# Nine products of lead for the two adding-DMA blocks of a Strassen group, and one more tile in the weight ring

## The chip, the cores and the metric

One NeuronCore of a Trainium2 chip runs the whole program in one launch. The metric is the device time of one execution in microseconds, lower is better; the median of three timed executions of the kernel before is 2247.82 us.

## The reference, cut to what matters

Two residual blocks over 512 tokens of width 1024, in fp32. The first holds an HGRN2 mixer and a dilated attention, each followed by a feed-forward network (FFN); the second a mixer of sparse attention and gated linear attention, and a third FFN. All three FFNs have this form, with `d_ff` 2816:

```python
def swiglu_ffn(u, w_in, w_down):
    gate, up = jnp.split(u @ w_in, 2, axis=-1)
    return (jax.nn.silu(gate) * up) @ w_down
```

`u` is the normalised state (512 x 1024), `w_in` is 1024 x 5632. So the up-projection gives 22 pairs of a gate tile and an up tile, each tile 128 columns wide.

## The kernel before, in words

**Arithmetic.** fp32 products are made of three fp32r matmuls. Each operand is split into a *head* (the value rounded to fp32r by ScalarE's CAST) and a *rest* (value minus head), and `mm3` sums rest times head, head times head and head times rest in PSUM. A weight block that is used must therefore stand in SBUF as a head and a rest.

**The three up-projections** (`ffn`). The first five pairs of a FFN (`FC`) are made by plain products through `gemm`. The other 17 (6 in the first half of the FFN, 11 in the second) are made by Strassen's method in groups, one pair each (`strassen`). A group has seven products, a1, b1, a2, b2, c, a3, a4, each with its own 128 x 512 weight block (a linear combination of the four quarters) and 12 matmuls of 128 x 256. The order is written out as slots in `S_AT`: a1 0, b1 1, a2 3, b2 4, c 5, a3 6, a4 9, so that a4 of a group stands at slot 2 of the next; the last group of a half goes by `S_LAST`: a1 0, b1 1, a2 3, b2 4, a3 5, c 6, a4 7. There are 51 groups, 357 products, 4284 matmuls. The products a1 to a4 of a group accumulate in one PSUM bank; behind each, ScalarE copies the bank out (behind a1 and a2, `COPY G`), or VectorE reads it. `b2` and `c` are added into `G` by VectorE and put through silu by ScalarE.

**The weights** (`Weights`). A group's blocks come from three loads on SP's queue: r4 (512 KB, two quarters), r1 and r3 (256 KB each). VectorE makes the sums from them with five adds (`sums_1`, `sums_2`: adds 1 and 2 into the second halves of r1 and r3, adds 3 and 4 into r2). `heads(i)` is one 128 x 1024 CAST for two products, `rests(i)` their subtract on VectorE. For two products the rest is made in another way (`rest_dma`): ScalarE writes the negated head, and a DMA issued by GpSimd adds the raw block from HBM to it (line 339; 256 KB, 102 of them). These two are c and a4. So heads(3) casts c and a3 together, and rests(3) issues c's DMA and subtracts for a3; `last` makes a4's block.

**The order of the preparation.** Each step stands in a list with a due time: the slot of the product that uses it, less a lead, in steps of `SLOT` (1.44 us). Before a product is issued, `advance` issues all that is due; a step issues first the loads of its group that are not yet issued. The leads before: sums 7 and 6 ahead of a1, heads(1) 5, rests(1) 4, heads(2) and rests(2) 6 and 5 ahead of a2, heads(3) and rests(3) 6 and 5.9 ahead of c, `last` at a1 itself. All tiles (128 x 1024 fp32) come from one ring of `ROOM` = 12; a load that takes a used tile waits until the last use of that tile is over. Instructions of an engine run in the order in which they were issued, so a load that waits holds up the loads behind it on SP's queue.

Most element-wise instructions are recorded at one line (L249, a helper), so the rows are told apart by engine and by the program's tile names: `w_raw` is a raw block, `w` a head or a rest, `G` and `h` the gate and up results, `ps` a PSUM bank, `E` the activations' operands.

Of the kernel before, what the change touches and what calls it, by code (L numbers as in the profile page):

```python
# [78 lines left out]
def strassen_order(n):  # L79

    at = [(7 * g + t, g, p) for g in range(n) for p, t in (S_AT if g < n - 1 else S_LAST).items()]
    return [(g, p) for _, g, p in sorted(at)]
# [101 lines left out]
class Clock:  # L184
# [3 lines left out]
    def __init__(self, hop):  # L188
        self.hop = hop
        self.free = {"pe": 0.0, "v": 0.0, "a": 0.0, "g": 0.0}  # L190
        self.written, self.read = {}, {}
        self.held = []
# [68 lines left out]
class Weights:  # L261
# [1 line left out]

    ROOM, HELD = 12, 3
    TILE, SLOT = 0.68, 1.44

    def __init__(self, prog, ctx, aps):
# [71 lines left out]
    def group(self, grp):  # L341
        n, aps, t, split, at, v = grp["n"], grp["aps"], grp["tiles"], grp["split"], grp["at"], self.v
        first, second = slice(0, n), slice(n, 2 * n)

        def load(name, sl, ap):
            def go():
                t[name] = self.tile(F32)
                self.nc.sync.dma_start(t[name][:, sl], ap)
            return go

        def add(o, osl, x, xsl, y, ysl):
            v.tensor_add(t[o][:, osl], t[x][:, xsl], t[y][:, ysl])

        def sums_1():
            add("r1", second, "r4", second, "r4", first)
            add("r3", second, "r1", first, "r4", second)

        def sums_2():
            t["r2"] = self.tile(F32)
            add("r2", first, "r1", first, "r1", second)  # L360
            add("r2", second, "r3", first, "r2", first)

        def heads(i):
            def go():
                t["h%d" % i] = self.tile()
                self.a.copy(t["h%d" % i][:, :2 * n], t["r%d" % i][:, :2 * n])
            return go

        def rests(i):
            def go():  # L370
                h, l = t["h%d" % i], self.tile()
                t["l%d" % i] = l
                if i == 3:
                    self.rest_dma(l[:, first], h[:, first], aps[2])
                    self.sub(v, l[:, second], t["r3"][:, second], h[:, second])
                else:
                    self.sub(v, l[:, :2 * n], t["r%d" % i][:, :2 * n], h[:, :2 * n])
                self.free(t, "r%d" % i)
                for p, sl in zip(((), ("a1", "b1"), ("a2", "b2"), ("c", "a3"))[i], (first, second)):
                    split[p] = h[:, sl], l[:, sl]  # L380
            return go

        def last():
            t["l4"] = self.tile()
            hi, lo = t["l4"][:, second], t["l4"][:, first]
            self.a.copy(hi, t["r4"][:, first])
            self.rest_dma(lo, hi, aps[0][:, first])
            split["a4"] = hi, lo
            self.free(t, "r4")

        u = len(self.units)
        self.loads += [[load("r4", slice(0, 2 * n), aps[0]), u], [load("r1", first, aps[1]), u], [load("r3", first, aps[2]), u]]
        s = self.SLOT
        for use, lead, what in (
            ("a1", 7, sums_1), ("a1", 6, sums_2), ("a1", 5, heads(1)), ("a1", 4, rests(1)), ("a2", 6, heads(2)), ("a2", 5, rests(2)),
            ("c", 6, heads(3)), ("c", 5.9, rests(3)), ("a1", 0, last),
        ):
            self.todo.append((at[use] - lead * s + 0.01, u, what, len(self.loads)))

# [43 lines left out]

    def product(self, p):

        _, grp, name = self.units[self.at]
        assert p == name, (self.at, p, name)
        self.now = grp["at"][p]
        self.advance()
        r = grp["split"].pop(p)  # L450
        self.at += 1
        if p in ("b1", "b2", "a3", "a4"):
            self.free(grp["tiles"], *{"b1": ("l1", "h1"), "b2": ("l2", "h2"), "a3": ("l3", "h3"), "a4": ("l4",)}[p])
        return r


class Program:
    def __init__(self, tc, ctx, I, O):
        self.tc, self.nc, self.I, self.O = tc, tc.nc, I, O
        nc = self.nc  # L460
        self.clock = Clock(0.5)
        self.v, self.a = Timed(nc.vector, "v", self.clock), Timed(nc.scalar, "a", self.clock)
        self.g, self.t = Timed(nc.gpsimd, "g", self.clock), Timed(nc.tensor, "pe", self.clock)
        PS = bass.MemoryType.PSUM
        self.const = ctx.enter_context(tc.tile_pool(name="const", bufs=1))
        self.p2 = ctx.enter_context(tc.tile_pool(name="p2", bufs=28))
        self.p4 = ctx.enter_context(tc.tile_pool(name="p4", bufs=26))
        self.small = ctx.enter_context(tc.tile_pool(name="small", bufs=24))
        self.ps_p = ctx.enter_context(tc.tile_pool(name="ps", bufs=8, space=PS))
        self.bg, self.hooks, self.evq = [], deque(), []  # L470
        self.after_norm = None
# [60 lines left out]
    def mm3(self, out, a, b, first, last):  # L532

        self.t.matmul(out, a[1], b[0], start=first, stop=False, skip_group_check=True)
        self.t.matmul(out, a[0], b[0], start=False, stop=False, skip_group_check=True)
        self.t.matmul(out, a[0], b[1], start=False, stop=last, skip_group_check=True)

    def mm(self, out, a, b, first=True, last=True):
        self.t.matmul(out, a, b, start=first, stop=last, skip_group_check=True)
# [1048 lines left out]
    def strassen(self, X, afters):  # L1588


        banks = {}
        for g, p in strassen_order(len(afters)):
            key = g, p[0]
            first = key not in banks
            if first:
                banks[key] = self.ps((128, 256))
            hi, lo = self.W.product(p)
            for j in range(len(X)):
                sl = slice(128 * j, 128 * j + 128)
                self.mm3(banks[key], (hi[:, sl], lo[:, sl]), X[j][p], first and j == 0, j == len(X) - 1)  # L1600
            afters[g][p](banks[key])


# [83 lines left out]
    def finish(self, hh):  # L1687
# [41 lines left out]
        for k in range(FH):  # L1729
            product(0, k)  # L1730
        residual(0)
        for k in range(FH):
            product(1, k)
            if k == 3:
                rt = stats(0)
                v.reciprocal(rt, rt)
            if k == 6:
                f = spread(rt)
                store(0, f, 0)
# [153 lines left out]
```

## Time and profile before

| | |
|---|---|
| timed runs | 2247.82 us median of 3 (2245.15 to 2249.3) |
| profiled execution | 2243.74 us, its span 2242.0 us |
| TensorE busy (PE) | 2114.1 us, 94% of the span |
| VectorE (DVE), ScalarE (ACT), GpSimd (POOL) busy | 1358.9, 999.9, 507.0 us |
| DMA | 218 MB, 97 GB/s over the span |
| the matmuls of the Strassen groups | 546.8 us busy, 74.6 us idle ahead of them |

How to read it: TensorE's instructions are in order, so any idle time of TensorE lengthens the kernel unless another wait behind it would have come anyway. The profile puts down each idle stretch to what ended it, an instruction of another engine or the landing of a DMA. A row of a timeline gives the start and the length of a run of like instructions in us, the engine, the line, the operation with output and inputs, and in brackets how long the engine had waited, and for whom.

### The profile page before, as it was taken

To read this page: it belongs to the slowest core of one execution; us is meant where nothing else is said; L and a number is where in the kernel's file an instruction comes from. 1 tells how busy PE (TensorE), PEld (TensorE's weight loads), DVE (VectorE), ACT (ScalarE), POOL (GpSimd) and SP (SyncE) were. 2 spreads that over 40 slices of the span, in tenths; PEclk is the share of its full clock that TensorE was granted. 3 is DMA by queue.
4 is the path that set the end of the run, shared out by engine and by line. 5 is a ranking of instruction groups with operands and counts; after the bars stand their busy time and mean duration, and the time that the engine had idled before them with its cause. 6 is when DMAs were issued, how large, how long until landed. Compare 5 with 4: busy or idle time off the path is not lost. (4 is left out here: it accounts for less than half of the span.)

```text
span 2242.0 us, 30605 instructions
## 1 busy us (share of the span) xinstructions
PE 2114.1 (94%) x11819; PEld 1844.4 (82%) x11819; DVE 1358.9 (61%) x2402; ACT 999.9 (45%) x1750; POOL 507.0 (23%) x394
## 2 busy tenths in 40 slices
PE   9999999899989999999989989999799999989988
PEld 7787787888978998887888888887588787879977
DVE  4768858636744545547745754456678658635742
ACT  5343445514643333444533544244545644525633
POOL 4323321101112424231100113331511331101101
PEclk9999999999999999999999999999999999999999
DMA  5111231634653222222453662321121131533651
GB/s 201 66 57 48 66 132 49 165 92 99 145 147 104 85 76 76 76 87 78 99 150 78 137 163 92 117 85 45 48 67 57 57 102 56 140 114 95 150 142 47
DMA packets 77921, 218.07 MB, mean 97 GB/s; under 512 B 8704, under 2 KB 10768, under 8 KB 77776
## 3 DMA queue, kind: packets, MB, share of 16 engines
q1 hardware_dynamic: 60928, 183.86, 25.4%
q0 software_dynamic: 15696, 30.17, 8.1%
q8 instruction: 93, 1.52, 0.3%
q10 hardware_dynamic: 1152, 2.10, 0.3%
q14 instruction: 52, 0.43, 0.1%
HBM read 213.99 MB, written 2.10 MB: 96 GB/s over the span
## 5 line engine op out<-in xcount | busy, mean ns | idle before, releaser
L249 PE MATMUL ps<-u,w 128*128 128x512 f32 x2640 | 664.3, 401 | 8.1 <-DVE w L249 7.3
L249 PE MATMUL ps<-E,w 128*128 128x256 f32 x4284 | 546.8, 290 | 74.6 <-DMA w<-in_ffn 57.8
L249 PEld LDWEIGHTS ps<-E,w 128*128 128x128 f32 x4284 | 534.0, 197 | 88.0 <-DMA w<-in_ffn 66.3
L249 PEld LDWEIGHTS ps<-u,w 128*128 128x128 f32 x2640 | 485.7, 189 | 111.9 <-DVE w L249 10.7
L249 ACT CAST w<-w_raw 128x1024 fp32r<-128x1024 f32 (+2 forms) x448 | 438.5, 984 | 224.6 <-DVE w L249 113.4
L249 DVE TENSOR_TENSOR w<-w_raw,w 128x1024 fp32r<-128x1024 f32 (+2 forms) x323 | 386.9, 1200 | 205.9 <-ACT w L249 158.9
L249 PE MATMUL ps<-h,w 128*128 128x512 f32 (+1 forms) x1617 | 361.6, 385 | 0.5 <-DVE x L249 0.5
L249 PEld LDWEIGHTS ps<-h,w 128*128 128x128 f32 x1617 | 299.4, 188 | 60.9 <-DVE x L249 0.7
L249 POOL TENSOR_TENSOR w<-w_raw,w 128x1024 fp32r<-128x1024 f32 (+3 forms) x74 | 176.3, 2383 | 371.8 <-ACT w L249 288.7
L339 POOL DMA_DIRECT2D w<-in_ffn x102 | 88.6, 887 | 666.0 <-ACT G L249 281.6
L249 DVE TENSOR_TENSOR w_raw<-w_raw 128x512 f32<-128x512 f32 x204 | 135.5, 688 | 49.2 <-DMA w_raw<-in_ffn 47.6
L249 PE MATMUL ps<-w,u 128*128 128x512 f32 (+1 forms) x672 | 156.7, 389 | 1.8 <-DVE u L249 1.8
L249 DVE TENSOR_TENSOR x<-x,ps 128x512 f32<-128x512 f32 (+1 forms) x73 | 49.5, 679 | 164.0 <-PE ps L249 164.0
L249 PEld LDWEIGHTS ps<-w,u 128*128 128x128 f32 x672 | 135.2, 225 | 15.1 <-DVE u L249 2.2
L249 ACT ACTIVATE P<-P,nm 128x128 f32<-128x128 f32 (+2 forms) x112 | 55.2, 494 | 139.6 <-DVE nm L249 131.7
L249 POOL TENSOR_TENSOR sq_acc<-sq_acc,sq 128x512 f32<-128x512 f32 x48 | 65.0, 1360 | 230.5 <-ACT sq L249 230.4
L249 ACT CAST h<-h 128x512 fp32r<-128x512 f32 x66 | 40.9, 619 | 167.4 <-DVE h L249 167.4
L249 ACT ACTIVATE G<-G 128x256 f32<-128x256 f32 x102 | 42.4, 416 | 123.5 <-DVE G L249 123.4
L249 DVE TENSOR_TENSOR h<-h 128x512 fp32r<-128x512 f32 x66 | 45.7, 692 | 50.1 <-ACT h L249 50.1
L249 ACT ACTIVATE u<-x,vec 128x512 fp32r<-128x512 f32 x40 | 28.9, 722 | 102.6 <-DVE x L249 100.3
L249 DVE TENSOR_TENSOR G<-G,ps 128x256 f32<-128x256 f32 x102 | 39.3, 415 | 57.9 <-PE ps L249 57.9
L249 ACT ACT_TABLE_LOAD x49 | 62.9, 1283 | 19.3 <-DVE Pc L249 12.2
(295 smaller groups left out, 2276.2 us busy)
## 6 DMA issues: line engine op xcount, KB each, us to landing
w_raw<-in_ffn SPq DMA_DIRECT2D x147, 512.0 KB, 3.5
w_raw<-in_ffn SPq DMA_DIRECT2D x102, 256.0 KB, 2.7
w<-in_ffn POOLq DMA_DIRECT2D x102, 256.0 KB, 4.9
w_raw<-in_attn SPq DMA_DIRECT2D x48, 512.0 KB, 3.5
w_raw<-in_blk SPq DMA_DIRECT2D x47, 512.0 KB, 3.5
w_raw<-in_hgrn SPq DMA_DIRECT2D x36, 512.0 KB, 3.6
w_raw<-in_blk SPq DMA_DIRECT2D x7, 404.0 KB, 3.1
x<-in_xt SPq DMA_DIRECT2D x8, 256.0 KB, 5.3
```

The source lines that it names most:

```text
L249: r = f(*args, **kw)
L339: self.nc.gpsimd.dma_start(lo, ap, accum_op=ALU.add)
```

## The change

The blocks of c, a3 and a4 are prepared by a new step `alone`, each into a tile of its own with a 128 x 512 CAST: c with a lead of 9 products, a3 with 6, a4 with 9. For c and a4 the step goes on with `rest_dma`, for a3 with a subtract on VectorE. c's head and its DMA so move from slots 0 of the group's own a1 to slot 4 (b2) of the group before it. In a last group, c's DMA moves from slot 1 (b1) to two slots ahead of a1, and a4's from slot 1 to one slot ahead of a1 and behind c's. The ring has 13 tiles, and the pool `p4` gives up one of 26. Further, `strassen` declares each product's matmuls independent of the head's CAST, the first of three excepted, which reads the rest.

```diff
-    ROOM, HELD = 12, 3
+    ROOM, HELD = 13, 3
@@ group
-                self.a.copy(t["h%d" % i][:, :2 * n], t["r%d" % i][:, :2 * n])
+                made[i] = self.a.copy(t["h%d" % i][:, :2 * n], t["r%d" % i][:, :2 * n])
...
-                if i == 3:
-                    self.rest_dma(l[:, first], h[:, first], aps[2])
-                    self.sub(v, l[:, second], t["r3"][:, second], h[:, second])
+        def alone(p, name, src, sl, ap, done):
+            def go():
+                t[name] = self.tile()
+                lo, hi = t[name][:, first], t[name][:, second]
+                head = self.a.copy(hi, t[src][:, sl])
+                if ap is None:
+                    self.sub(v, lo, t[src][:, sl], hi)
                 else:
...
+                    self.rest_dma(lo, hi, ap)
+                split[p] = hi, lo, head
+                if done:
+                    self.free(t, src)
             return go
-        def last():
-            t["l4"] = self.tile()
-            hi, lo = t["l4"][:, second], t["l4"][:, first]
-            self.a.copy(hi, t["r4"][:, first])
-            self.rest_dma(lo, hi, aps[0][:, first])
-            split["a4"] = hi, lo
-            self.free(t, "r4")
...
-            ("c", 6, heads(3)), ("c", 5.9, rests(3)), ("a1", 0, last),
+            ("c", 9, alone("c", "c", "r3", first, aps[2], False)), ("a3", 6, alone("a3", "l3", "r3", second, None, True)),
+            ("a4", 9, alone("a4", "l4", "r4", first, aps[0][:, first], True)),
@@ Program
-        self.p4 = ctx.enter_context(tc.tile_pool(name="p4", bufs=26))
+        self.p4 = ctx.enter_context(tc.tile_pool(name="p4", bufs=25))
@@ strassen
+                for m in self.mm3(banks[key], (hi[:, sl], lo[:, sl]), X[j][p], first and j == 0, j == len(X) - 1):
+                    self.tc.declare_no_dep(m.ins, head.ins, reason="made before the rest that the first product waits for")
```

How the order of the instructions changes is shown at three places; numbers behind a name are buffers. The order of TensorE's instructions is the same in both programs.

ScalarE, an inner group in the second half of the first FFN. Before, `w_5001` is the head of c and a3 together, `w_5003` c's rest, `w_5025` a4's head and rest:

```order
L249 CAST w_4968<-w_raw_4917 128x1024
L249 ACTIVATE G_4890<-G_4890 128x256
L249 CAST w_5001<-w_raw_4900 128x1024
L249 ACTIVATE w_5003<-w_5001 128x512
L249 COPY G_5021<-ps_5000 128x256
L249 CAST w_5025<-w_raw_4876 128x512
L249 ACTIVATE w_5025<-w_5025 128x512
L249 COPY h_5022<-ps_5024 128x256
L249 CAST h_5064<-h_4891 128x512
```

Now, `w_4965` is c's head and rest, `w_5037` a3's, `w_5040` a4's:

```order
L249 COPY G_4901<-ps_4886 128x256
L249 CAST w_4965<-w_raw_4912 128x512
L249 ACTIVATE w_4965<-w_4965 128x512
L249 ACTIVATE G_4901<-G_4901 128x256
L249 CAST w_4984<-w_raw_4929 128x1024
L249 ACTIVATE G_4901<-G_4901 128x256
L249 COPY G_5033<-ps_5018 128x256
L249 CAST w_5037<-w_raw_4912 128x512
L249 CAST w_5040<-w_raw_4870 128x512
L249 ACTIVATE w_5040<-w_5040 128x512
```

c's two instructions stand behind the copy that follows a2 of the group before, ahead of its two silus; a3's CAST stands where the double CAST was.

ScalarE, the last group of that half. Before, `w_5545` is the head of c and a3, `w_5547` a4's, `w_5551` c's rest:

```order
L249 COPY G_5541<-ps_5524 128x256
L249 CAST w_5545<-w_raw_5424 128x1024
L249 CAST w_5547<-w_raw_5400 128x512
L249 ACTIVATE w_5547<-w_5547 128x512
L249 ACTIVATE w_5551<-w_5545 128x512
L249 COPY h_5542<-ps_5544 128x256
```

Now, `w_5510` is c's, `w_5530` a4's, `w_5551` a3's:

```order
L249 CAST w_5508<-w_raw_5457 128x1024
L249 CAST w_5510<-w_raw_5440 128x512
L249 ACTIVATE w_5510<-w_5510 128x512
L249 ACTIVATE G_5429<-G_5429 128x256
L249 CAST w_5530<-w_raw_5398 128x512
L249 ACTIVATE w_5530<-w_5530 128x512
L249 CAST w_5551<-w_raw_5440 128x512
L249 COPY G_5568<-ps_5550 128x256
L249 COPY h_5569<-ps_5571 128x256
```

Both rests are now ahead of the copy behind a1 of the last group, and c's ahead of a4's.

SP, the loads of two groups in the first FFN, each r4, r1 and r3, with the semaphores that each waits for (PE is TensorE's, DVE VectorE's, DMASW that of a GpSimd DMA, DMAHW that of SP's own). Before:

```order
L348 DMA w_raw_4876<-in_ffn0 128x1024 [waits DMASW4_49,DMAHW3_49,DVE_49,PE_49]
L348 DMA w_raw_4898<-in_ffn0 128x512 [waits DMAHW1_49,DVE_49]
L348 DMA w_raw_4900<-in_ffn0 128x512 [waits DMAHW2_49,PE_49]
L348 DMA w_raw_5007<-in_ffn0 128x1024 [waits DMASW6_49,DMAHW6_49,DVE_49,PE_49]
L348 DMA w_raw_5029<-in_ffn0 128x512 [waits DMAHW4_49,DVE_49]
L348 DMA w_raw_5031<-in_ffn0 128x512 [waits DMAHW5_49,PE_49]
```

Now:

```order
L349 DMA w_raw_4870<-in_ffn0 128x1024 [waits DMASW4_49,DMAHW0_49,DMASW1_49,PE_49]
L349 DMA w_raw_4887<-in_ffn0 128x512 [waits DMAHW1_49,DMASW4_49,PE_49]
L349 DMA w_raw_4912<-in_ffn0 128x512 [waits DMAHW2_49,DVE_49]
L349 DMA w_raw_5002<-in_ffn0 128x1024 [waits DMAHW3_49,DMASW3_49,PE_49]
L349 DMA w_raw_5019<-in_ffn0 128x512 [waits DMAHW4_49,DMASW6_49,PE_49]
L349 DMA w_raw_5044<-in_ffn0 128x512 [waits DMAHW5_49,DVE_49]
```

With 13 tiles the three loads take other tiles: VectorE's rests(2) were waited for by r1's load and now are by r3's; r1's waits for the end of product c, r4's for the end of b2.

On GpSimd, the first group's c DMA of each FFN now stands ahead of the last of the five multiplies that make `sg`, the gate tiles of the plain pairs, by the norm's factor; before, it stood behind all five. VectorE's instructions are the same but for a3's subtract and a few reorderings at the ends of the halves.

## Rows read from the trace of the kernel before

**Rows 1.** Costliest groups on the page: busy us, mean ns, idle us before, its main releaser.
```profile
L249 PE MATMUL ps<-E,w 128*128 128x256 f32 x4284 | 546.8, 290 | 74.6 <-DMA w<-in_ffn 57.8
```
**Rows 2.** TensorE's waits in the whole span: waiter, releaser, sum in us, count, largest.
```profile
PE ps L249 <- DMA w<-in_ffn: 57.8, 39, 6.8
...
PE ps L249 <- ACT G L249: 15.0, 12, 2.6
```
**Rows 3.** Timeline of TensorE, one group period in a steady stretch.
```profile
611.81 10.33 PE L249 MATMUL ps<-E,w 128*128 128x256 f32 x84 [0.63 <-DMA w<-in_ffn]
```
**Rows 4.** Timeline of VectorE over the same period.
```profile
604.99 1.23 DVE L249 TENSOR_TENSOR w<-w_raw,w 128x1024 fp32r<-128x1024 f32 x1 [1.09 <-ACT w L249]
...
607.53 0.68 DVE L249 TENSOR_TENSOR w_raw<-w_raw 128x512 f32<-128x512 f32 x1
608.93 2.02 DVE L249 TENSOR_TENSOR w_raw<-w_raw 128x512 f32<-128x512 f32 x3 [0.72 <-DMA w_raw<-in_ffn]
...
614.06 0.75 DVE L249 TENSOR_TENSOR G<-G,ps 128x256 f32<-128x256 f32 x2
...
615.90 1.23 DVE L249 TENSOR_TENSOR w<-w_raw,w 128x1024 fp32r<-128x1024 f32 x1 [1.09 <-ACT w L249]
```
**Rows 5.** Timeline of ScalarE and GpSimd over the same period.
```profile
606.24 0.63 ACT L249 ACTIVATE w<-w 128x512 fp32r<-128x512 f32 x1
...
611.32 0.62 ACT L249 CAST h<-h 128x512 fp32r<-128x512 f32 x1 [2.74 <-DVE h L249]
611.84 1.05 ACT L249 CAST w<-w_raw 128x1024 fp32r<-128x1024 f32 x1
614.51 0.42 ACT L249 ACTIVATE G<-G 128x256 f32<-128x256 f32 x1 [1.36 <-DVE G L249]
...
607.47 0.87 POOL L339 DMA_DIRECT2D w<-in_ffn  x1 [8.80 <-ACT G L249]
```
**Rows 6.** DMA issues with KB each and median us to landing: 600 to 615 us.
```profile
w_raw<-in_ffn SPq DMA_DIRECT2D x2, 256.0 KB, 2.7
w<-in_ffn POOLq DMA_DIRECT2D x2, 256.0 KB, 4.8
```
**Rows 7.** The same view, 526 to 536 us.
```profile
w_raw<-in_ffn SPq DMA_DIRECT2D x1, 256.0 KB, 6.3
```
**Rows 8.** Timeline of TensorE: the last 24 matmuls of the first and the last half.
```profile
450.96 5.49 PE L249 MATMUL ps<-E,w 128*128 128x256 f32 x24 [6.25 <-DMA w<-in_ffn]
...
2165.01 5.27 PE L249 MATMUL ps<-E,w 128*128 128x256 f32 x24 [6.28 <-DMA w<-in_ffn]
```
**Rows 9.** Timeline of TensorE: 24 such matmuls at a half's start.
```profile
1076.57 3.13 PE L249 MATMUL ps<-E,w 128*128 128x256 f32 x24 [0.52 <-DVE w L249]
```
**Rows 10.** Timeline, last group of the second half: the ACTIVATEs and DMAs of a4 and c.
```profile
629.31 1.15 ACT L249 ACTIVATE w<-w 128x512 fp32r<-128x512 f32 x2
...
630.24 1.75 POOL L339 DMA_DIRECT2D w<-in_ffn  x2 [9.69 <-ACT w L249]
```
**Rows 11.** DMA issues, 628 to 645 us.
```profile
w_raw<-in_ffn SPq DMA_DIRECT2D x6, 512.0 KB, 5.3
w<-in_ffn POOLq DMA_DIRECT2D x2, 256.0 KB, 8.2
```
**Rows 12.** Windows: us, busy PE, PEld, DVE, ACT, POOL, granted clock, DMA share, GB/s.
```profile
638.00:640.00 2.00, 0.00 (x0) 0.00 (x0) 0.00 (x0) 0.00 (x0) 0.00 (x0) 0.50 0.98 309
620.50:622.00 1.50, 1.50 (x14) 1.44 (x13) 1.47 (x4) 0.00 (x0) 0.05 (x1) 1.00 1.03 139
```
**Rows 13.** Timeline, start of the second FFN: TensorE, VectorE, GpSimd.
```profile
1082.13 4.10 PE L249 MATMUL ps<-E,w 128*128 128x256 f32 x32 [2.43 <-ACT G L249]
...
1080.48 0.68 DVE L249 TENSOR_TENSOR h<-ps,sg 128x512 f32<-128x512 f32 x1
...
1076.19 1.48 POOL L249 TENSOR_TENSOR sg<-sg,r_bc 128x512 f32<-128x512 f32 x1 [10.61 <-ACT sg L249]
```
**Rows 14.** Timeline, second group of the first FFN's second half: VectorE.
```profile
533.08 0.69 DVE L249 TENSOR_TENSOR w_raw<-w_raw 128x512 f32<-128x512 f32 x1 [2.65 <-DMA w_raw<-in_ffn]
```

More of the change, by code (lines that the diff above doesn't have):

```diff
@@ L343, in group @@
         first, second = slice(0, n), slice(n, 2 * n)
+        made = {}
         def load(name, sl, ap):
@@ L372, in go @@
                 t["l%d" % i] = l
-                if i == 3:
-                    self.rest_dma(l[:, first], h[:, first], aps[2])
-                    self.sub(v, l[:, second], t["r3"][:, second], h[:, second])
-                else:
[L377 to L380, printed above, removed]
-            return go
-        def last():
-            t["l4"] = self.tile()
-            hi, lo = t["l4"][:, second], t["l4"][:, first]
-            self.a.copy(hi, t["r4"][:, first])
-            self.rest_dma(lo, hi, aps[0][:, first])
-            split["a4"] = hi, lo
-            self.free(t, "r4")
+                self.sub(v, l[:, :2 * n], t["r%d" % i][:, :2 * n], h[:, :2 * n])
+                self.free(t, "r%d" % i)
+                for p, sl in zip(((), ("a1", "b1"), ("a2", "b2"))[i], (first, second)):
+                    split[p] = h[:, sl], l[:, sl], made[i]
+            return go
+        def alone(p, name, src, sl, ap, done):
[5 more added lines that the diff above has]
+                    self.sub(v, lo, t[src][:, sl], hi)
+                else:
+                    self.rest_dma(lo, hi, ap)
+                split[p] = hi, lo, head
+                if done:
+                    self.free(t, src)
+            return go
         u = len(self.units)
@@ L451, in product @@
         self.at += 1
-        if p in ("b1", "b2", "a3", "a4"):
-            self.free(grp["tiles"], *{"b1": ("l1", "h1"), "b2": ("l2", "h2"), "a3": ("l3", "h3"), "a4": ("l4",)}[p])
+        if p in ("b1", "b2", "c", "a3", "a4"):
+            self.free(grp["tiles"], *{"b1": ("l1", "h1"), "b2": ("l2", "h2"), "c": ("c",), "a3": ("l3",), "a4": ("l4",)}[p])
         return r
@@ L534, in mm3 @@
         self.t.matmul(out, a[1], b[0], start=first, stop=False, skip_group_check=True)
-        self.t.matmul(out, a[0], b[0], start=False, stop=False, skip_group_check=True)
-        self.t.matmul(out, a[0], b[1], start=False, stop=last, skip_group_check=True)
+        m = self.t.matmul(out, a[0], b[0], start=False, stop=False, skip_group_check=True)
+        return m, self.t.matmul(out, a[0], b[1], start=False, stop=last, skip_group_check=True)
     def mm(self, out, a, b, first=True, last=True):
@@ L1596, in strassen @@
                 banks[key] = self.ps((128, 256))
-            hi, lo = self.W.product(p)
+            hi, lo, head = self.W.product(p)
             for j in range(len(X)):
                 sl = slice(128 * j, 128 * j + 128)
-                self.mm3(banks[key], (hi[:, sl], lo[:, sl]), X[j][p], first and j == 0, j == len(X) - 1)
+                for m in self.mm3(banks[key], (hi[:, sl], lo[:, sl]), X[j][p], first and j == 0, j == len(X) - 1):
+                    self.tc.declare_no_dep(m.ins, head.ins, reason="made before the rest that the first product waits for")
             afters[g][p](banks[key])
```

## The prediction, made before the changed kernel was run

> **What bounds the kernel now.** I read first the page's costliest groups. The Strassen matmuls are busy for 546.8 us and have 74.6 us of idle TensorE ahead of them, 57.8 of it ended by an adding DMA [rows 1]. TensorE is busy 94% of the span, so what can be won here is this idle time and what it does to the clock. Second, TensorE's waits: 39 waits for the adding DMAs with 57.8 us, the largest 6.8, and 12 for ScalarE's copy into `G` with 15.0 us [rows 2]. Third, where they stand. Six of the 39 are the last c of a half, just ahead of the last 24 matmuls (c and a4): 6.25 in the first half, 6.28 in the last [rows 8], and with the four between them (5.50, 5.47, 5.86, 6.83) 36.2 us. The other 33 sum to 21.6, some 0.65 each; a typical one is the 0.63 ahead of 84 matmuls [rows 3], also at c. So there are two stages, the six ends of halves and the steady groups between.
>
> Fourth, the clock at the ends. The 24 matmuls behind such a wait take 5.27 to 5.49 us [rows 8]; the same number takes 3.13 at a half's start [rows 9]. While TensorE stands still in the wait, the granted clock reads 0.50, that is 1.2 GHz [rows 12], and the matmuls behind it begin at that level.
>
> Fifth, what a steady group is bound by. TensorE needs 10.33 us for 84 matmuls [rows 3], but rests(2) of one group and of the next are 10.91 apart (604.99 to 615.90) [rows 4]. The reader is to see a loop without TensorE in it. rests(2) frees the tile that the next r1 load takes; 2.54 us after it begins come adds 1 to 4, the second of which waits 0.72 for that load; then the head of `h`, the double CAST at 611.84, the adds into `G` at 614.06, the silu at 614.51, and rests(2) again [rows 4, 5]. It keeps c's DMA (issued 607.47 [rows 5], landing 4.8 later [rows 6]) just too late for TensorE, which pays the difference of 10.91 and 10.33 at c in each group.
>
> **The change, part by part.** Durations are of the profiled execution, 2243.74 us, which is 4.08 under the median of 2247.82; I subtract from the one and add 4.08.
>
> *Ends of halves.* At the end shown, both ACTIVATEs run from 629.31, both DMAs are issued at 630.24, a4's first and c's behind it [rows 10], and they take 8.2 us in the median [rows 11], which as a mean of two is about 7.2 for the first and 9.3 for the second. Six loads of 512 KB are issued in that stretch [rows 11]. Now c's DMA goes out three slots earlier: a slot is 10.33 / 7 = 1.48 us [rows 3], so 4.4 us; and it is the first of the two, which by 9.3 - 7.2 gives 2.1 more: 6.5 of a wait of 5.5 to 6.8. a4's goes out two slots, 2.95 us, earlier, but as the second; it is needed a slot after c. Its landing moves from 630.24 + 7.2 = 637.4 to 630.24 - 2.95 + 9.3 = 636.6 at worst, against a need near 635 (639.5, when the late one landed, less the 5.9 to 6.8 of wait, plus 1.48), so it is up to 1.5 late, or not at all if it takes 7.2. I leave 1.0 at each end: 36.2 - 6 x 1.0 = **30.2** gained. Bounds: 0 left, and 3.5 left, if the loads still delay the second DMA by another 2 us.
>
> *Clock at the ends.* With no long wait the 24 matmuls should run at full clock: 6 x 3.13 = 18.8 in place of 30.8 (the six measured: 5.49, 4.90, 4.90, 5.49, 4.71, 5.27): **12.0**. Bounds: 0, if 2 us or more of wait are left, and 12.0.
>
> *Steady groups.* c's head and negation leave the place behind a1's copy and run four slots, 5.9 us, earlier, so c's landing is far ahead of its need. Does the loop get shorter too, or does another product wait then? r1's load no longer waits for rests(2), so the 0.72 of waiting leaves the loop: 10.91 - 0.72 = 10.19, under TensorE's 10.33. TensorE then bounds the group, with 0.14 to spare. In the loop's other parts ScalarE gets c's CAST (0.62, as the CAST of `h` of the same size) and ACTIVATE (0.63) between the double CAST and the silus: from 611.84 to 614.51 there are 2.67 us, of which the double CAST is 1.05 and 1.36 were waiting for VectorE [rows 5]; 1.25 goes into 1.36 with 0.1 left. On balance ScalarE works 0.2 us more a group (0.62 + 0.62 in place of 1.05), beside idle time, so 0. If that cover were gone, silu and with it the loop would be later by what does not fit, some 0.2 us x 39 inner groups = 8 us: the lower bound. I take **18.6** of the 21.6: 3 us stay for the groups next to a half's start and end, where the order is not yet steady. Bounds: -8 (above), and 21.6.
>
> *r3's load.* It is now r3's load that waits for rests(2), and add 4 needs it. Without the 0.72, add 4 begins 2.54 + 3 x 0.65 = 4.48 after rests(2) begins (adds by the 2.02 us of three [rows 4], begun a little closer than busy time says). The load is issued at 1.23 and takes L. The loop through it is 1.23 + L + (10.19 - 4.48) = L + 6.94. With 2.7, the two SP loads of this size in a steady stretch [rows 6], it lands with 0.55 to spare, and 10.33 is not reached until L = 3.39. The longest such load took 6.3, beside two adding DMAs [rows 7]; the shortest bound is 2.7. I take 2.7: in the new order c's DMA is on the way from about slot 5.5 to 8.5 of the group before (issue 2.2 us behind the start of b2, then 4.4), a4's from 9.6 to 12.6, and rests(2) ends near slot 8.2, so that the load falls mostly between them. What L = 2.7 rests on is a rival below.
>
> Against this stands a row on the adding DMAs themselves: in 620.50 to 622.00 the 16 DMA engines are fully taken (share 1.03) while only 139 GB/s move [rows 12]. The Trainium skill, "DMA: Bandwidth & Descriptors", section on queues, rings and completion order, says that each DMA engine takes turns between the queue rows that have work, a packet at a time. By that rule a plain load beside an adding DMA gets half of the engines' time; the trace agrees with row 7, and with rows 6 only if the two seldom meet.
>
> *Copies into G.* Of 15.0 us, three starts of a FFN hold 7.4 (2.43 at the second [rows 13]): there the plain pairs' `h` at 1080.48 comes late on VectorE, which the change leaves as it is. The other nine sum to 7.6; behind them are adds that wait for a load beside adding DMAs, as the 2.65 [rows 14]. c's DMA now goes out ahead of that crowd: **5.6** gained, bounds 0 and 7.6.
>
> *The rest.* GpSimd's c DMA ahead of the last `sg` multiply (0.87 us [rows 5]) moves the multiply's end from 1077.67 to 1078.5; its reader begins at 1080.48 [rows 13]: 0. The dropped dependence of products on the heads: the rest is made from the head, so the first matmul's wait covers it: 0, bounds 0 either way, as TensorE's other matmuls carried no wait. The pool with a tile less: its peak is 25 tiles (8 of `u`, 12 operands, 5 `h`): 0.
>
> Sum: 30.2 + 12.0 + 18.6 + 5.6 = 66.4; 2243.7 - 66.4 = 2177.3 in the profile, **2181** as a median.
>
> **Rivals.** (A) The wait moves from c to a3 or a1, and the steady groups keep their 10.91, since r3's load takes about 4.0 us (4.0 + 6.94 = 10.94). For it: row 7, and that the load leaves a place between transfers for one near c's DMA; against it: 2.7 in the steady stretch. Only the ends are won: 2247.8 - 42.2 = 2206. Chance 0.20. (B) The ends keep 2.5 us of wait each and the low clock, as both DMAs still run beside six loads of 512 KB: 36.2 - 15 = 21.2, with 18.6 and 5.6 45.4, so 2202. Chance 0.07. (C) Slower: r3's load and c's adding DMA run side by side in every inner group and the load doubles to 5.4. The group then takes 12.34, 1.43 more than now, x 39 = 56 lost against 42.2 won at the ends: 2262; with 6.3 it would be 2297. It decides from L = 5.05, where 39 x (L - 3.97) equals 42.2. For it: row 7; against it: r1's load was 2.7 although an adding DMA was issued 1.3 us into it [rows 5, 6]. The Trainium skill's rule of turns, cited above, is this mechanism. Chance 0.05. (D) The change does nothing, because something else (the raw block's load) holds c's CAST where it was: 2248, chance 0.02.
>
> **How the numbers follow.** Forecast 0.66, rivals 0.20, 0.07, 0.05, 0.02. Faster than now by over 0.2% (4.5 us, about what a measurement can tell from none): 0.66 + 0.20 + 0.07 = 0.93; same 0.02; slower 0.05. The forecast's own range: all of the bounds' best gives 36.2 + 12.0 + 21.6 + 7.6 = 77.4, or 2170, a little less for what shorter waits may do to the clock elsewhere: 2167. On the other side it reaches past rivals A and B, with 4 us for their own spread: 2210.
>
> **What would show it.** Right: at the ends, waits under 1.5 us and 24 matmuls in about 3.1 us; waits for the adding DMAs under 10 us in all; rests(2) 10.3 us apart; r3's load landing before add 4. Wrong: rests(2) still 10.9 or more apart and TensorE waiting at a1, a2 or a3 for VectorE's rests; a `w_raw` load of 256 KB with a median over 3.4 us; add 4 waiting for `in_ffn` in most groups; a second wait at a4 in the ends.

## The result, and the profile after

The changed kernel takes 2175.47 us (median of 4, 2173.09 to 2178.41) against 2247.88 us before (4 runs, 2245.15 to 2249.3): ratio 0.968, 95% interval 0.9663 to 0.9697. Forecast were 2181 us, in 2167 to 2210. The profiled execution's span is 2174.4 us, 67.6 less than the 2242.0 before.

The page's groups of the changed kernel that answer to [rows 1], with the adds and the DMAs:

```profile
L249 PE MATMUL ps<-E,w 128*128 128x256 f32 x4284 | 526.6, 285 | 26.9 <-ACT G L249 11.8
...
L249 DVE TENSOR_TENSOR w_raw<-w_raw 128x512 f32<-128x512 f32 x204 | 132.6, 687 | 9.7 <-DMA w_raw<-in_ffn 8.0
...
w_raw<-in_ffn SPq DMA_DIRECT2D x102, 256.0 KB, 3.2
w<-in_ffn POOLq DMA_DIRECT2D x102, 256.0 KB, 4.1
```

Before, the same matmuls had 546.8 us busy and 74.6 idle [rows 1]. 20.2 less busy and 47.7 less idle make 67.9, so the whole gain of 67.6 stands in this one row, and the other rows changed by little in sum. TensorE's waits, as in [rows 2]:

```profile
PE ps L249 <- ACT G L249: 11.8, 6, 2.8
PE ps L249 <- DMA w<-in_ffn: 10.3, 9, 1.9
```

The waits for adding DMAs fell from 57.8 to 10.3, their count from 39 to 9. Where those nine are, TensorE's timeline shows; here the two halves of the second FFN, each from its start or nearly so to its end:

```profile
1058.73 56.66 PE L249 MATMUL ps<-E,w 128*128 128x256 f32 x456 [2.80 <-ACT G L249]
1116.04 1.69 PE L249 MATMUL ps<-E,w 128*128 128x256 f32 x12 [0.64 <-DMA w<-in_ffn]
1118.97 1.66 PE L249 MATMUL ps<-E,w 128*128 128x256 f32 x12 [1.24 <-DMA w<-in_ffn]
1180.33 87.98 PE L249 MATMUL ps<-E,w 128*128 128x256 f32 x732
1269.13 20.82 PE L249 MATMUL ps<-E,w 128*128 128x256 f32 x168 [0.82 <-ACT G L249]
1291.35 1.69 PE L249 MATMUL ps<-E,w 128*128 128x256 f32 x12 [1.39 <-DMA w<-in_ffn]
1294.06 1.67 PE L249 MATMUL ps<-E,w 128*128 128x256 f32 x12 [1.02 <-DMA w<-in_ffn]
```

All nine are at ends of halves: at four ends one ahead of c and one ahead of a4, as here, and one at a4 of another end; before, each end had one of 5.5 to 6.8 at c [rows 8]. A tenth wait of this kind is the 1.68 us at the last a4 of the program: the profile names VectorE there, but a4's DMA landed 0.14 us before that product began, 8.3 us after its issue. 732 matmuls run with no wait at all, 87.98 / 732 x 84 = 10.10 us a group; before, each group of 84 took 10.33 and 0.63 of wait [rows 3]. So TensorE's own need was not 10.33: the row after a wait carries some 0.23 us more, seen again in 12 matmuls behind a wait (1.69) against 12 in a stream (1.44, from 87.98 / 732 x 12). On VectorE, rests(2) of two groups (the first and the last row; columns as in [rows 4]):

```profile
587.41 1.23 DVE L249 TENSOR_TENSOR w<-w_raw,w 128x1024 fp32r<-128x1024 f32 x1 [1.09 <-ACT w L249]
...
591.15 1.41 DVE L249 TENSOR_TENSOR w_raw<-w_raw 128x512 f32<-128x512 f32 x2
...
597.51 1.23 DVE L249 TENSOR_TENSOR w<-w_raw,w 128x1024 fp32r<-128x1024 f32 x1 [1.09 <-ACT w L249]
```

597.51 - 587.41 = 10.10, the same as TensorE's group, and the adds at 591.15 don't wait for a load. Not every group is so: in 12 of the 51, add 4 (the last of the four adds that a group has: 204 in 51 groups) waits for r3's load, 7.5 us in all. The three longest of these waits (1.84, 1.69 and 1.10 us) stand shortly ahead of the three waits for a copy that are not at a start. Of one such group, VectorE's add 4 and the wait that TensorE has 3 us later, at a3:

```profile
2053.96 0.69 DVE L249 TENSOR_TENSOR w_raw<-w_raw 128x512 f32<-128x512 f32 x1 [1.69 <-DMA w_raw<-in_ffn]
...
2056.91 42.64 PE L249 MATMUL ps<-E,w 128*128 128x256 f32 x348 [1.26 <-ACT G L249]
```

Between the two, VectorE's part of `h` is late behind add 4, then ScalarE's CAST of `h`, which waited 4.19 us for it, and behind that the copy for which a3 waits. At the end of the second half of the first FFN the windows show the clock, with the columns of [rows 12]:

```profile
616.00:618.00 2.00, 1.14 (x9) 1.14 (x10) 0.53 (x2) 0.34 (x1) 0.00 (x0) 1.00 1.05 311
618.00:620.00 2.00, 1.04 (x9) 0.87 (x8) 1.40 (x2) 0.42 (x1) 0.00 (x0) 1.00 1.05 418
```

The granted clock stays at 1.00 through both short waits; before it read 0.50 at this end [rows 12]. It is not so at every end: behind the single wait of 1.86 us at the end of the first half it fell, and the 12 matmuls there took 2.86 us in place of about 1.7:

```profile
443.80 2.86 PE L249 MATMUL ps<-E,w 128*128 128x256 f32 x12 [1.86 <-DMA w<-in_ffn]
```
```profile
444.00:446.00 2.00, 2.00 (x10) 2.00 (x11) 0.00 (x0) 0.00 (x0) 0.00 (x0) 0.50 1.03 404
```

### The profile page after: what moved, and what is told of

It is laid out like the page before. It is cut to its first block, busy times and chain, and to the rows that moved or that the text cites. A ratio compares the mean times of both kernels' runs of the same rounds, so it can differ in the third digit from the quotient of the medians.

```text
span 2174.4 us, 30621 instructions
## 1 busy us (share of the span) xinstructions
PE 2096.1 (96%) x11819; PEld 1833.6 (84%) x11819; DVE 1355.4 (62%) x2402; ACT 1010.0 (46%) x1801; POOL 507.9 (23%) x394
## 4 chain that ended last, share of the span: by engine, by line
PE 68%; DVE 16%; ACT 5%; issue 5%; DMA 4%; POOL 1%; SPq 0%; DVEq 0%; POOLq 0%; ACTq 0%
PE ps L249 68%; DVE E L249 3%; DVE w L249 2%; ACT w L249 2%; DMA w<-in_ffn 2%; DVE Q L249 2%; DVE Sd L249 2%; DMA w_raw<-in_ffn 1%; DVE w_raw L249 1%; DVE h L249 1%; DVE P L249 1%; ACT h L249 1%; DVE K L249 0%; DVE gs L249 0%; ACT L249 0%
## 5 line engine op out<-in xcount | busy, mean ns | idle before, releaser
L249 PE MATMUL ps<-E,w 128*128 128x256 f32 x4284 | 526.6, 285 | 26.9 <-ACT G L249 11.8
L249 ACT CAST w<-w_raw 128x1024 fp32r<-128x1024 f32 (+2 forms) x499 | 444.6, 904 | 225.2 <-DVE w L249 133.5
L249 PEld LDWEIGHTS ps<-E,w 128*128 128x128 f32 x4284 | 521.0, 193 | 33.1 <-ACT G L249 14.9
L249 PE MATMUL ps<-ao,w 128*128 128x512 f32 x288 | 68.0, 393 | 1.3 <-ACT ao L249 1.3
L249 ACT ACTIVATE w<-w 128x512 fp32r<-128x512 f32 x102 | 64.5, 632 | 3.2
```

What stands on the lines that cost most here:

```text
L249: r = f(*args, **kw)
```

## The experiments

Theory 1, built on the prediction's account of the loop, says that the inner groups were bound by the loop through r1's load, which the 13th tile frees from rests(2), and that c's lead serves the ends of the halves above all. Its rival says that c's adding DMA bound each group by the place it was issued from, and that its lead of nine won the groups. The change does both at once, so I took them apart.

**ring13: the kernel before with only the ring.**

```diff
-    ROOM, HELD = 12, 3
+    ROOM, HELD = 13, 3
-        self.p4 = ctx.enter_context(tc.tile_pool(name="p4", bufs=26))
+        self.p4 = ctx.enter_context(tc.tile_pool(name="p4", bufs=25))
```

> The kernel before with only the ring of 13 tiles (and 25 in p4); c, a3 and a4 are prepared as before. Theory 1 (the prediction's): a steady group was bound by the loop through r1's load, which waits for rests(2); with that wait gone everything behind it, c's DMA too, comes 0.72 us earlier, so the steady groups run at 10.1 to 10.4 us, c's waits of 21.6 us go to under 6, the ends keep 6 us of wait each: about 2218 to 2225. Rival: c's adding DMA itself bound the group by when it was issued, and the loop had slack behind it: nothing moves, 2244 to 2250, and TensorE still waits some 0.6 us at each c.

Measured: 2197.53 us, ratio 0.9773 (0.9736 to 0.981), more than either theory gave. Two page rows, two of TensorE's waits, and of its timeline a whole half with its end:

```profile
L249 PE MATMUL ps<-E,w 128*128 128x256 f32 x4284 | 533.3, 288 | 43.2 <-DMA w<-in_ffn 34.2
...
L249 DVE TENSOR_TENSOR w_raw<-w_raw 128x512 f32<-128x512 f32 x204 | 133.0, 687 | 3.4 <-DMA w_raw<-in_ffn 1.1
```
```profile
PE ps L249 <- DMA w<-in_ffn: 34.2, 8, 6.3
...
PE ps L249 <- ACT G L249: 7.4, 3, 2.6
```
```profile
1065.13 56.43 PE L249 MATMUL ps<-E,w 128*128 128x256 f32 x456 [2.43 <-ACT G L249]
1127.03 4.41 PE L249 MATMUL ps<-E,w 128*128 128x256 f32 x24 [5.46 <-DMA w<-in_ffn]
```

456 matmuls without a wait: with c's steps where they always were, the inner waits are all but gone (8 waits left, 33.6 us of the 34.2 in the six ends). The nine copy waits outside the starts are gone too, and VectorE's adds wait 1.1 us for loads where they waited 47.6 before: 23.2 at add 2 for r1's load, 11.6 at add 1 for r4's, 12.8 at add 4 for r3's. So the tile freed all three loads, r1's by the most; they were not tried apart. Theory 1 stands; its number left out the copy waits (7.6 us) and the 0.23 us that each of the 33 waits and the nine copy waits cost the matmuls behind it, some 10 us. By the spans of the two profiles the gain is 44 us (2242.0 to 2197.9), by the ratio 51; the profiles don't show the difference.

**ring12_early: the change without the 13th tile.**

```diff
-    ROOM, HELD = 13, 3
+    ROOM, HELD = 12, 3
-            ("c", 9, alone("c", ... )), ("a3", 6, alone("a3", ...
+            ("c", 6 if grp["first"] else 9, alone("c", ... )), ("a3", 6.9 if grp["first"] else 6, alone("a3", ...
...
```

Left out of the edit here: `first` is set where the groups are made, and in a last group c's tile is given back together with a3's.

> The change with a ring of 12 tiles; in the first group of a half c keeps its old place, for there 12 tiles don't hold it. r1's load waits for rests(2) again. Theory 1: c is early, but the loop through r1's load still takes 10.9 us, so TensorE waits some 0.6 us a group at another product (a rest of VectorE's): 2200 to 2210. Rival (c's DMA alone bound the group): 2174 to 2180, rests(2) 10.1 us apart.

Measured: 2221.62 us, ratio 0.9875 (0.9846 to 0.9904), slower than both numbers. The page's rows and the largest wait of TensorE:

```profile
L249 PE MATMUL ps<-E,w 128*128 128x256 f32 x4284 | 534.3, 286 | 58.2 <-ACT G L249 48.1
...
L249 DVE TENSOR_TENSOR w_raw<-w_raw 128x512 f32<-128x512 f32 x204 | 136.1, 688 | 55.5 <-DMA w_raw<-in_ffn 50.1
```
```profile
572.69 10.32 PE L249 MATMUL ps<-E,w 128*128 128x256 f32 x84 [1.76 <-ACT G L249]
583.79 10.34 PE L249 MATMUL ps<-E,w 128*128 128x256 f32 x84 [0.78 <-ACT G L249]
```
```profile
590.94 2.02 DVE L249 TENSOR_TENSOR w_raw<-w_raw 128x512 f32<-128x512 f32 x3 [1.24 <-DMA w_raw<-in_ffn]
```

c is early, no inner wait for an adding DMA is left, and a group still takes 11.1 us: the wait has only changed its name, to the copy behind a2, for which a3 waits. add 2 waits 1.24 us for r1's load where it waited 0.72 [rows 4]. Why it waits longer than before was not tried apart; c's DMA is now on the way at that time. What is won in this run is the ends.

**ends_only: the change, c of the inner groups at its old lead.** Here and below, `end` is true for the last group of a half.

```diff
-            ("c", 9, alone("c", ...
+            ("c", 9 if end else 6, alone("c", ...
```

> The change, but c of every inner group is prepared at lead 6, where it was before; the last groups and the ring of 13 as in the change. Theory 1: with r1's load free of rests(2) the inner groups need c's lead little: 2176 to 2186. Rival (c's lead is what won the inner groups): 2200 to 2210, with some 0.6 us of wait at each inner c.

Measured: 2186.48 us, ratio 0.9726 (0.9696 to 0.9757), between the two. In the profile the matmuls have 528.8 us busy and 28.4 idle, in place of 526.6 and 26.9; nine waits at inner c's come back, 0.18 to 1.61 us each, 6.2 in sum, and the copy waits in inner groups go. By span it is 2181.0 against 2174.4. So with the ring given, c's inner lead is worth some 7 us by span and 11 by the medians, and what the run has beyond ring13, the last groups' leads above all, 17 by span and 11 by the medians. VectorE's adds no longer wait for a load at all in this run (1.8 us idle, none of it put down to a load): it is c's lead that brings those waits into the change.

**head_waits: the change with the products' dependence on the head kept.**

```diff
-                for m in self.mm3(...):
-                    self.tc.declare_no_dep(m.ins, head.ins, reason=...)
+                self.mm3(...)
```

> The change without the declaration that products don't depend on the head's CAST. The prediction costs it at nothing, since the first matmul's wait for the rest covers it: 2173 to 2178. Rival (it saves waits of TensorE's sequencer, 357 products by some 0.02 us): 2180 to 2185.

Measured: 2175.32 us, ratio 0.9676 (0.9648 to 0.9704). The declaration is worth nothing here. The run is also a second measurement of the change, and its profile shows how far two such differ: 524.0 busy and 24.3 idle.

**a4_late: the change without a4's lead.**

```diff
-            ("a4", 9, alone("a4", ...
+            ("a1", 0, alone("a4", ...
```

> The change with a4's lead undone: its step is due at a1 again, so in a last group at slot 1 and not 1 ahead of a1 (inner groups keep their place). Theory: a4's DMA is issued some 2.95 us later at each end, so the wait at a4 goes from 1.0 to 3 to 4 us there and the matmuls behind it start at 1.2 GHz: 2188 to 2202. Rival (the second of the two DMAs is held by the six 512 KB loads, not by its issue): 2174 to 2182.

Measured: 2184.85 us (2174.61 to 2186.68), ratio 0.97 (0.9674 to 0.9726): not clear of the change. The profile shows why it is so little: at five ends a4 waits 2.1 to 3.1 us (12.9 in all), and c's own wait is gone. Two waits of about 1 us became one of 2.6. So a4's early DMA seems to delay c's, which the theory, with c's wait unchanged, didn't have. The time lies between the two expectations, and at four of the six ends the granted clock fell to 0.50 behind a4's wait.

**ends_11: two slots more for c and a4 in the last groups.**

```diff
-            ("c", 9, alone("c", ...      ("a4", 9, alone("a4", ...
+            ("c", 11 if end else 9, alone("c", ...      ("a4", 11 if end else 9, alone("a4", ...
```

> The change with lead 11 for c and a4 in the last groups only, two slots or 2.95 us earlier. Theory: the waits at the ends, 0.6 to 1.9 us each, go: 2162 to 2169. Rival: the DMAs go out earlier but meet the group's own loads and adds there, and something else waits: 2173 to 2180.

Measured: 2164.93 us, ratio 0.9624 (0.96 to 0.9649), as the theory gave, but not as cheaply as it said: no wait for an adding DMA is left, and the copy waits rise from 11.8 to 20.8. Each end now has one of 0.9 to 2.6 us, at a3 of the last group but one, which waits for the copy behind a2: c's and a4's CASTs and ACTIVATEs stand earlier on ScalarE, which is likely the same cause as in the next run.

**inner_10: lead 10 for c in the inner groups.**

```diff
-            ("c", 9, alone("c", ...
+            ("c", 9 if end else 10, alone("c", ...
```

> The change with lead 10 for c in the inner groups. Theory: c's lead of 9 is long enough there (no inner wait for an adding DMA is left), so one more gives nothing: 2173 to 2178. Rival: c's DMA, further ahead of r3's load, ends the adds' 8 us of waiting for loads and the 3.6 us of waits for copies behind them: 2168 to 2172.

Measured: 2194.97 us, ratio 0.9753 (0.9736 to 0.9769): 20 us lost by one slot in the medians, 16 by the ratios, foreseen by neither. ScalarE's timeline, and TensorE's at the same place:

```profile
578.14 1.56 ACT L249 CAST w<-w_raw 128x1024 fp32r<-128x1024 f32 x2
579.74 0.63 ACT L249 ACTIVATE w<-w 128x512 fp32r<-128x512 f32 x1
580.27 0.35 ACT L249 COPY G<-ps 128x256 f32<-128x256 f32 x1
```
```profile
559.16 10.33 PE L249 MATMUL ps<-E,w 128*128 128x256 f32 x84 [0.43 <-ACT G L249]
569.92 10.33 PE L249 MATMUL ps<-E,w 128*128 128x256 f32 x84 [0.43 <-ACT G L249]
580.68 10.33 PE L249 MATMUL ps<-E,w 128*128 128x256 f32 x84 [0.42 <-ACT G L249]
```

c's CAST (the second of the x2) and ACTIVATE now stand ahead of the copy behind a2, for which a3 waits; in the change they stand behind it. a3 waits 0.42 us in group after group, and each wait costs the matmuls behind it 0.23 more: 10.76 us a group instead of 10.10.

**ends_sub: VectorE makes the rests of c and a4 in the last groups.**

```diff
-            ("c", 9, alone("c", "c", "r3", first, aps[2], ...
-            ("a4", 9, alone("a4", "l4", "r4", first, aps[0][:, first], True)),
+            ("c", 6 if end else 9, alone("c", "c", "r3", first, None if end else aps[2], ...
+            ("a4", 6 if end else 9, alone("a4", "l4", "r4", first, None if end else aps[0][:, first], True)),
```

> The change, but in the six last groups c's and a4's rests are subtracted by VectorE at lead 6 in place of the adding DMAs. Theory: what is left at the ends, 10.3 us of waits for adding DMAs and 1.7 for the last a4, goes, and with it some 0.25 us that each wait costs the matmuls behind it: 2160 to 2166. Rival: 1.4 us more of VectorE at each end make its sums late, and TensorE waits there for VectorE: 2172 to 2182.

Measured: 2154.96 us (2152.95 to 2157.35), ratio 0.9577 (0.9563 to 0.9592), the fastest of all and 5 us under the theory's best. One page row, and the same half as above, now with its end:

```profile
L249 PE MATMUL ps<-E,w 128*128 128x256 f32 x4284 | 520.6, 284 | 13.0 <-ACT G L249 11.3
```
```profile
1052.07 59.35 PE L249 MATMUL ps<-E,w 128*128 128x256 f32 x480 [2.78 <-ACT G L249]
```
```profile
606.20 1.89 DVE L249 TENSOR_TENSOR w<-w_raw,w 128x512 fp32r<-128x512 f32 x3
```

The 480 matmuls include c and a4 of the last group. The price is in the last row: two subtracts more for VectorE at each end (x3, with a3's), 1.3 us, which no product waits for. Against the change the row has 13.9 us less idle and 6.0 less busy, which is where the gain lies. Of the copy waits that stay, 8.2 us are in the three starts, and three are single waits of about 1 us.

**sub_inner6 and sub_inner8: that version with other inner leads for c.**

```diff
-            ("c", 6 if end else 9, alone("c", ...
+            ("c", 6, alone("c", ...
...
+            ("c", 6 if end else 8, alone("c", ...
```

> The version with VectorE's rests at the ends, and c's inner lead back at 6, where the kernel before had it. If c's lead is worth 5 to 10 us in the inner groups (the change against the run with the ends alone), 2160 to 2166, with some single waits of 0.2 to 1.6 us at c. Rival (that difference came from the ends and from scatter): 2153 to 2158.

> The same with lead 8: c's CAST and ACTIVATE stand behind the CAST of heads(2) and ahead of the group's last silu. Theory (any place from which the DMA lands in time, that isn't ahead of a1's copy, does): within 3 us of lead 9, 2152 to 2158. Rival: the silu is 1.25 us later and a4's part of h with it, so the loop is longer than TensorE's: 2165 to 2200.

Measured: lead 6 2171.29 us, ratio 0.9679 (0.9654 to 0.9703), outside of both expectations; lead 8 2161.65, ratio 0.9629 (0.9608 to 0.9649), behind lead 9 by some 7 us in the medians and 0.5% in the ratios, also outside of both. In the profile of lead 6, five of TensorE's waits at an inner c are of 3 us and more, two of them here:

```profile
1233.47 32.07 PE L249 MATMUL ps<-E,w 128*128 128x256 f32 x252 [3.84 <-DMA w<-in_ffn]
1268.62 27.30 PE L249 MATMUL ps<-E,w 128*128 128x256 f32 x204 [3.08 <-DMA w<-in_ffn]
```
```profile
w_raw<-in_ffn SPq DMA_DIRECT2D x2, 256.0 KB, 4.3
w<-in_ffn POOLq DMA_DIRECT2D x2, 256.0 KB, 8.3
w_raw<-in_ffn SPq DMA_DIRECT2D x1, 512.0 KB, 7.3
```

The second block is the DMA view of that run for 1224 to 1234 us: two adding DMAs took 8.3 us beside three loads, in place of 4.8 [rows 6]. But this profile is of an execution that took 2185.14 us, the longest of six; the others took 2166.99 to 2173.66. So the five waits can't all stand in the others too, and what the median of lead 6 lost against lead 9 is not shown. What the profile does show is how late an adding DMA can be, and that lead 6 leaves no room for it. For lead 8 the profile has the busy time 7 us higher than at lead 9 (527.6 against 520.6) with as little idle (12.3). Some 2.6 us of that stand at the start of the third FFN, where the granted clock reads 0.51 from 1855 to 1862 us and the 29 matmuls take 6.1 us; at the same start the profile of lead 9 reads 1.00. Where the rest comes from was not settled.

## Why the prediction was right, step by step

- **What binds a steady group.** Right, and shown by ring13 and ring12_early: the loop rests(2), r1's load, adds, and back. With the ring alone the waits go; with c's lead alone they stay under another name. But the prediction booked the 18.6 us under c's lead and named the ring as what lets it through. It is the other way round: of the 72 us, the ring takes about 51 alone by the ratio (0.9773; 44 of 67.6 by the spans), and c's inner lead 7 to 11 on top. The loop, put at 10.19 without its wait, can't have been longer than the 10.10 that rests(2) were apart.
- **TensorE's need of 10.33 us.** This is the term that was mis-sized. 10.33 was read from rows that each begin behind a wait [rows 3]; the undisturbed group takes 10.10. With it the busy time fell by 20.2 us where the prediction had 12.0, for the clock at the ends alone. At four ends the 24 matmuls take 1.7 + 1.7 = 3.4 us in two pieces, against 4.7 to 5.5 before, so the ends gave at most about 30.8 - 6 x 3.4 = 10; the other 10 or so are from the inner groups.
- **Ends of halves.** 6.0 us were to stay, about 12 did: 10.3 for the adding DMAs, all at ends, and the 1.68 at the last a4, which is a4's DMA too. The step that failed is c's own term. Its wait was to go whole, for 4.4 us of earlier issue and 2.1 of a faster transfer make 6.5 against 5.5 to 6.8; but 0.6 to 1.4 us stayed at four ends. At the end shown in the windows above, c's DMA and its product are these two rows:

```profile
609.05 0.87 POOL L339 DMA_DIRECT2D w<-in_ffn  x1 [7.67 <-DVE w L249]
...
616.86 1.70 PE L249 MATMUL ps<-E,w 128*128 128x256 f32 x12 [1.21 <-DMA w<-in_ffn]
```

  TensorE was ready for c at 615.65 (616.86 - 1.21), 6.6 us after the issue at 609.05. Before, the DMA was issued at 630.77 and TensorE was ready at 634.60 (640.10 less the wait of 5.50), 3.8 us after it. So three slots in the order of the instructions gave 2.8 us and not 4.4: on ScalarE c's CAST begins behind the 128 x 1024 CAST of heads(2), and its ACTIVATE ends only at 608.76. The transfer took 7.8 us (609.05 to 616.82) in place of 9.3, 1.5 us less and not 2.1. 2.8 + 1.5 = 4.3 of 5.5 leaves the 1.2 that was measured. That a4 would be about 1 us late was right. With it came, at four ends, the second wait at a4 that the prediction had named as a sign of being wrong.
- **Inner waits for adding DMAs.** 3.0 were to stay, none did.
- **Copies into G.** 5.6 forecast, 3.2 measured. The starts grew from 7.4 to 8.2; of the other 7.6, 3.6 stayed, in the change but not in ring13, where all went. So the earlier c DMA doesn't help here, contrary to the prediction; it costs 3 to 4 us, for the adds wait 8.0 us for loads with it and 1.1 (ring13) or nothing (ends_only) without, and the three copy waits stand behind the longest of these.
- **r3's load**, on which rival A and the slower rival C hung: L was taken as 2.7. The 256 KB loads have a median of 3.2 us; r3's alone have 3.1, under the 3.39 up to which the sum hides them and far under 5.05. But 15 of the 51 took longer than 3.39 (11 before), up to 5.3, and these brought 6.7 of the 7.5 us that add 4 waited. So what rival A named did happen, in some groups and not in all. From 584 to 595 us, two 256 KB loads take 3.4 beside two adding DMAs, not twice 2.7. By the turn-taking between queues that the Trainium skill states ("DMA: Bandwidth & Descriptors", section on queues, rings and completion order), 5.4 is an estimate for a load that runs beside an adding DMA, twice the 2.7 of [rows 6]. Single loads in this trace come near it (5.3), but the median of the 256 KB loads is a fifth more, and a load of r3 that had adding DMAs on the way from its issue to its landing (537.83 us) took 3.1.
- **ScalarE's 0.1 us to spare** was worked out for the silus, and at lead 9 the work does hide. What inner_10 ran into is not in the prediction: the same two instructions ahead of a copy cost 16 to 20 us.
- **The rest at nothing**: the declared independence was measured at nothing (head_waits). The pool and GpSimd's order were not tried apart, but nothing of the 67.6 us is missing.

In sum: -1.3 us for the DMA waits, -2.4 for the copies, -3.0 for waits in VectorE's name that came new (1.68 of it the last a4), +8.2 for the busy time; 66.4 + 1.5 = 67.9. The mechanism was right, but that the total came so close is in part luck: 6.7 us too much in the waits and 8.2 too little in the busy time nearly cancel.

## What to carry to other kernels

When one product waits a little in every round, find the loop that sets the period before moving that product's input: here a load that waited for a free tile set it, and one tile more in the ring was worth some two thirds of the gain, while the earlier transfer alone only moved the wait to another product. Read an engine's own need from a stretch in which it never waits; rows that start behind a wait are too long. And a transfer with a scattered landing time is best taken out where it is needed soonest, if an engine has room for the work: 1.3 us of VectorE at each end won some 20 us more.

## What the runs showed of the hardware that was not expected

- A wait costs more than its idle time, at a granted clock of 1.00 too: 84 matmuls took 10.33 us behind a wait of 0.4 to 0.7 us, and 10.10 in a stream of 732. The records of the matmuls overlap (their ends are the profile's model): in the group of [rows 3] each lasts 0.28 us and they begin 0.12 apart, so the row of a run carries the last 0.16 us of its last matmul, which in a stream lies under the next one; and the second matmul behind the wait begins 0.22 us after the first, not 0.12.
- A 256 KB adding DMA landed after 4.1 us in the median in the changed kernel, and after 8.3 beside the loads at an end (604 to 622 us). There the loads were slow too: nine of 512 KB took 7.4 us in the median, in place of 3.6 for all 147 of this size in the FFNs. Over all groups the 256 KB loads went from 2.7 to 3.2 in the median with c's earlier DMA (2.7 in ring13 and in ends_only, where it is not earlier in the inner groups), with single ones up to 5.4.
